# One block inversion moved from VectorE to GpSimd, its follow-up steps pinned in the issue order, and the filler work dealt out anew, in a two-layer hybrid transformer kernel

## Chip, cores and metric

One core of a Trainium2 chip. The metric is the device time of one launch in microseconds (us), taken on the slowest core, here the only one. Inputs and outputs are float32; the weights are read from HBM once per launch.

## What is computed

Two layers over 256 latent tokens and 256 context tokens, model width 1024. Each layer has a modulation (six vectors out of one matrix product with the conditioning), a mixer of three branches (A: delta rule, B: gated linear attention, C: differential attention), a gated merge, and a feed-forward part (dense in layer 0, eight experts in layer 1). Cut to what matters here:

```python
mod_l = jnp.split((silu(c) @ w_mod[l] + b_mod[l])[:, None, :], 6, axis=-1)   # and mod_c from c_ctx
hl = _modulate(xl, norm1_g[l], mod_l[0], mod_l[1])
...
# branch A, per head and chunk of 64 tokens
lmat = jnp.tril(jnp.einsum('bhnid,bhnjd->bhnij', kb, k) * decay, -1)
tinv = lax.linalg.triangular_solve(eye + lmat, eye, left_side=True, lower=True, unit_diagonal=True)
u = tinv @ (v * beta)
w = tinv @ (kb * jnp.exp(gc)[..., None])
...
# merge
(ga * (ya @ w_o_a) + gb * (yb @ w_o_b) + gd * (yd @ w_o_c)) @ w_out          # gates: sigmoid(h @ w_in part)
```

What the change is about is `tinv`, the inverse of a unit lower triangular 64x64 matrix, of which a layer needs many.

## The kernel before

**Matmuls.** Every large product is made three times over (`mm3`, L272 to L274): both operands are split into a high and a low part, and high by high, high by low and low by high are summed in PSUM. A weight tile of 1 MB is loaded into one of three "raw" buffers (`load`, L248); its high part is a cast on ScalarE (ACT, L267), its low part a subtraction on VectorE (DVE, L268), four pieces of 128x512 to a load, put in a ring called "hl" (tiles `whl`). One load feeds two groups of 24 matmuls, of 512 columns where both token halves are wanted and of 256 where only the latents are (layer 1's gates).

**The order of the work.** A scheduler lays out the program by the order in which the code asks for things, one queue per engine, each carried out in its order. In `mixer` that order is a string, `PLAN` (L27, L28), one for each layer. Its words are stages: "pr" prepares the delta rule (matrices U, one for each direction), "iv" inverts (`a_inv`), "sc" is its scan, "gaN", "gbN", "gcN" are N loads' worth of the sigmoid gates of the three branches, computed ahead and parked in HBM, "za" the output gate of branch A, "qkB", "vB", "dec", "gla" branch B, "qC", "kC", "vC", "dif" branch C, "ha" to "hc" the heads' outputs and "ma" to "mc" the merges. "mN" stands for N units of modulation for later use.

**Modulation units.** `mod_unit` loads 1 MB of `w_mod` into a raw buffer and runs 8 matmuls on it (L348; 16 records in the trace) without a split, so its raw buffer is free only when the matmuls are done. Four units make a group in one PSUM tile; `mod_put` then copies the tile (ACT, L356, `modr`), transposes it by two matmuls (L359) and adds the bias (DVE, L366). The generator `mods` (L364 on) deals out the units; with `behind=0` a group's `mod_put` stands right behind its last unit. At the start of the program `run` takes eight units in groups of two, tag "c" (tile `rawc`), and between them the squares and row sums of the two token halves x (`norm_only`, L420 to L425, L432).

**The inversion.** `a_inv` gathers the 32x32 diagonal blocks of all matrices of a layer in one tile (128 partitions, 32x32), L642 and L644, makes N of them (L648) and solves by 31 steps of substitution (L653 a product, L655 a subtraction, over at most 256 elements a partition, in place in Y). Then it puts the result together: a copy (L657), a predicated copy (L658), two transposes (L659, L660), four copies back to U on ACT and four on DVE (L665, L667), a memset of Q on GpSimd (POOL, L669) and eight copies into Q (L675, L677). `a_join` (L680 on) goes from blocks of 32 to 64 by small matmuls (L699 on), and the scan follows.

The functions that the diff touches, as they stood:

Of the kernel before, what the change touches and what calls it, by code (L numbers as in the profile page):

```python
# [2 lines left out]

# [1 line left out]

# [18 lines left out]
MOE_RAW = (1, 0, 0)  # L24
MOE_PART = 3
PRE = (7,)
PLAN = ("sm ap su pr iv ga4 m4 za sc m16 dec qkB gb1 ha ma vB gla qC kC m4 gc1 vC hb dif mb hc mc",  # L27
        "sm ap pr ga1 m8 iv sc za m6 ga3 m1 gc1 qkB dec vB ha ma gla qC kC m1 vC hb dif mb hc mc")  # L28
MOE_PRE = 9
MOE_AT = 0  # L30
PART = 512
# [165 lines left out]
class Prog:  # L197
# [44 lines left out]
    def load(self, src, shape, tag="raw"):  # L242
# [5 lines left out]
        self.nc.sync.dma_start(r, src.rearrange("p (a b) -> p a b", a=n))  # L248
        return r

    def part(self, v):

        nc = self.nc
        n, size = v.shape[1], v.shape[2]
        step = -(-n // -(-n * size // PART))
        H, L = [], []
        for k in range(0, n, step):
            m = min(step, n - k)
            t = self.st.tile([128, 2, m, size], F32R, name="whl", tag="hl", bufs=2 * N_HL)
            self.split(t[:, 0], t[:, 1], v[:, k:k + m])  # L260
            H += [t[:, 0, i] for i in range(m)]
            L += [t[:, 1, i] for i in range(m)]
        return H, L
# [104 lines left out]
    def mods(self, groups, tag="raw", behind=1):  # L368

        last = []  # L370
        for l, us in groups:
            p = self.pm()
            for i, u in enumerate(us):
                self.mod_unit(l, u, i, len(us), p, tag)
                if i < len(us) - 1:
                    yield
            last.append((l, us, p))
            if len(last) > behind:
                self.mod_put(*last.pop(0))
            yield  # L380
        for v in last:
            self.mod_put(*v)

# [244 lines left out]
    def a_inv(self, s):  # L628

        nc = self.nc  # L630
        U = s["U"]
        W1 = self.ch([2, 32, 32], "W1")
        W2 = self.ch([2, 32, 32], "W2")
        Dg, M, N, Y = W1[:, 0], W1[:, 1], W2[:, 0], W2[:, 1]
        nc.gpsimd.memset(Y, 0.0)
        nc.gpsimd.memset(Y.rearrange("p i j -> p (i j)")[:, 0:1024:33], 1.0)
        quad = [slice(b * 32, (b + 1) * 32) for b in range(4)]
        for d in range(2):
            for b, r in enumerate(quad):
                src, dst = U[d][r, :, r], Dg[r, :, 16 * d:16 * d + 16].rearrange("p i m -> p m i")  # L640
                if b % 2:
                    nc.vector.tensor_copy(dst, src)  # L642
                else:
                    nc.scalar.copy(dst, src)  # L644
        nc.vector.transpose(M, Dg)
        dmb = self.dmask[:, :, None].to_broadcast([128, 32, 32])
        nc.scalar.copy(N, M)
        nc.vector.copy_predicated(N, dmb, M.rearrange("p i j -> p j i"))  # L648
        for c in range(31):
            a, b = 31 - c, c + 1  # L650
            tmp = self.sm([512], "fs")
            tv = tmp[:, :a * b].rearrange("p (a b) -> p a b", a=a)
            nc.vector.tensor_mul(tv, N[:, c + 1:, c:c + 1].to_broadcast([128, a, b]),  # L653
                                 Y[:, c:c + 1, :b].to_broadcast([128, a, b]))
            nc.vector.tensor_sub(Y[:, c + 1:, :b], Y[:, c + 1:, :b], tv)  # L655
        Z, Ps, Qs = M, Dg, N
        nc.scalar.copy(Z, Y)  # L657
        nc.vector.copy_predicated(Z, dmb, Y.rearrange("p i j -> p j i"))  # L658
        nc.vector.transpose(Ps, Z)  # L659
        nc.vector.transpose(Qs, Z.rearrange("p i j -> p j i"))  # L660
        for d in range(2):
            for b, r in enumerate(quad):
                dst, src = U[d][r, :, r], Ps[r, :, 16 * d:16 * d + 16].rearrange("p i m -> p m i")
                if b % 2:
                    nc.vector.tensor_copy(dst, src)  # L665
                else:
                    nc.scalar.copy(dst, src)  # L667
        Q = W1.rearrange("p a i j -> p (a i j)").rearrange("p (d m j) -> p d m j", d=2, m=16)
        nc.gpsimd.memset(Q, 0.0)  # L669
        for d in range(2):  # L670
            for b, r in enumerate(quad):
                c = slice((b % 2) * 32, (b % 2) * 32 + 32)
                dst, src = Q[r, d, :, c], Qs[r, :, 16 * d:16 * d + 16].rearrange("p i m -> p m i")
                if b % 2:
                    nc.vector.tensor_copy(dst, src)  # L675
                else:
                    nc.scalar.copy(dst, src)  # L677
        self.a_join(U, Q)

    def a_join(self, U, Q):  # L680

# [758 lines left out]
    def mixer(self, l, H):  # L1440

        self.todo = self.mods(MOD_AHEAD[l], behind=0)
        T, m = {}, []
        gn = lambda n: self.P(f"gn{n}{l}") if n != "c" else self.A["gnc", l]
        zu = {"a": U_ZA, "b": U_RB, "c": None}
        for w in PLAN[l].split():
            if w == "su":
                self.setup2()
            elif w == "sm":
                self.small_proj(l, H)  # L1450
            elif w == "ap":
                self.a_proj(l, H)
            elif w == "pr":
                T["s"] = self.a_prep(l)
            elif w == "iv":
                self.a_inv(T["s"])
            elif w == "sc":
                T["oa"] = self.a_scan(l, T["s"])
            elif w == "qkB":
                T[w] = self.gla_qk(l, H)  # L1460
            elif w in ("vB", "vC"):
                T[w] = self.values(l, U_VB if w == "vB" else U_VC, H, w)
            elif w == "dec":
                self.gla_decays(l)
            elif w == "gla":
                T["ob"] = self.gla(l, T["qkB"], T["vB"])
            elif w == "qC":
                T[w] = self.diff_qk(l, H, w, U_QC, 256 * l, 0.125)
            elif w == "kC":
                T[w] = self.diff_qk(l, H, w, U_KC, 0, 1.0)  # L1470
            elif w == "dif":
                T["oc"] = self.diff(l, T["qC"], T["kC"], T["vC"])
            elif w[0] == "z":
                self.stashed[l, w] = self.z_ahead(l, zu[w[1]], H, gn(w[1]), w[1])
            elif w[0] == "g":
                self.gates_ahead(l, "abc".index(w[1]), H, int(w[2:] or 4))
            elif w[0] == "h":
                T["y" + w[1]] = self.head_out(l, T["o" + w[1]], gn(w[1]), H, zu[w[1]], w[1])
            elif w in ("ma", "mb", "mc"):
                first = not m  # L1480
                m = m or self.wide(l, "m")
                self.merge(l, "abc".index(w[1]), H, T["y" + w[1]], m, first)
            else:
                for _ in range(int(w[1:])):
                    next(self.todo, None)
        return m
# [86 lines left out]
```

## Time and profile before

| what | value |
| --- | --- |
| median of 3 runs | 2606.64 us (2603.16 to 2609.61) |
| the profiled execution | 2607.5 us, its span 2605.7 us |
| PE (TensorE) busy | 2455.8 us, 94% of the span |
| DVE busy | 1718.3 us, 66% |
| ACT busy | 1417.3 us, 54% |
| POOL busy | 87.6 us, 3% |
| read from HBM | 463.65 MB, 181 GB/s over the span |
| mean granted clock of PE | 0.962 of full |

Busy time is the sum over an engine's instructions. Times inside the span count from its start. An engine's idle time costs something only if PE, or what PE waits for, is behind it. The granted clock of a stretch is 1.00 at the higher level (2.4 GHz) and 0.50 at the lower (1.2 GHz); between them the stretch had some of each.

### The profile page before, as it was taken

Reading aid. Unit: us, or ns where it says so; the run is one execution under the profiler, and the core shown is the slowest. Engines: PE = TensorE matmul, PEld = TensorE weight load, DVE = VectorE, ACT = ScalarE, POOL = GpSimd, SP = SyncE. Lnnn points to the kernel's source line nnn. Section 1 sums busy time; section 2 is a strip of 40 time slices with the busy share of each in tenths; the row PEclk is TensorE's granted clock in tenths of the full one; section 3 lists DMA queues with packets and bytes.
Section 4 is the critical chain, followed back from the end, with each engine's and each line's share of the span. In section 5 each row is a group of like instructions: output and inputs, shape, how many; then the busy total and the mean of one; then the engine's idle time right before and its main releaser. Section 6 shows DMA issues by size and latency. Waiting matters only on the chain.

```text
span 2605.7 us, 35872 instructions
## 1 busy us (share of the span) xinstructions
PE 2455.8 (94%) x13712; PEld 1979.8 (76%) x13712; DVE 1718.3 (66%) x3130; ACT 1417.3 (54%) x2352; POOL 87.6 (3%) x216
## 2 busy tenths in 40 slices
PE   5998999999998999998979999998999999999997
PEld 3786777677677788886859878787878888878876
DVE  4675446655644533335686475767988888988987
ACT  3764343225553432334845432666878777777775
POOL 0000001110010000000000010010000000000000
PEclk8998999989999999998978999998999999999998
DMA  6323632022132223222273130246979899999994
GB/s 248 110 93 149 246 132 71 17 106 81 49 128 83 81 77 121 96 74 89 97 271 115 46 141 33 89 169 261 386 270 365 332 350 351 346 347 353 342 366 181
DMA packets 72707, 473.13 MB, mean 182 GB/s; under 512 B 8208, under 2 KB 10384, under 8 KB 19664
## 3 DMA queue, kind: packets, MB, share of 16 engines
q1 hardware_dynamic: 68208, 464.73, 48.1%
q10 hardware_dynamic: 4320, 6.03, 0.6%
q8 instruction: 110, 1.80, 0.3%
q14 instruction: 69, 0.57, 0.1%
HBM read 463.65 MB, written 7.08 MB: 181 GB/s over the span
## 4 chain that ended last, share of the span: by engine, by line
PE 85%; DVE 8%; ACT 4%; issue 2%; DMA 1%; SPq 0%; POOL 0%; ACTq 0%; DVEq 0%; POOLq 0%
PE pm L273 19%; PE pm L272 19%; PE pm L274 19%; PE y L274 3%; PE y L273 3%; PE y L272 3%; PE la L985 2%; PE pm L348 2%; PE pq L1052 1%; DVE ATb L987 1%; PE pm L844 1%; PE ob L996 1%; PE tp L1352 1%; DMA raw<-in_wmod_dram 1%; DVE zq L973 1%
## 5 line engine op out<-in xcount | busy, mean ns | idle before, releaser
L268 DVE TENSOR_TENSOR whl<-raw,whl 128x512 fp32r<-128x512 f32 (+2 forms) x490 | 331.2, 682 | 341.0 <-ACT whl L267 338.0
L272 PE MATMUL pm<-hh,whl 128*128 128x512 f32 (+2 forms) x1264 | 477.7, 380 | 13.0 <-ACT whl L267 6.6
L274 PE MATMUL pm<-hh,whl 128*128 128x512 f32 (+2 forms) x1264 | 467.7, 371 | 12.3 <-DVE whl L268 12.3
L267 ACT CAST whl<-raw 128x512 fp32r<-128x512 f32 (+2 forms) x490 | 289.8, 600 | 339.9 <-PE pm L274 268.7
L273 PE MATMUL pm<-hl,whl 128*128 128x512 f32 (+2 forms) x1264 | 470.9, 373 | 0.0
L268 DVE TENSOR_TENSOR wp<-rawc,wp 128x1024 fp32r<-128x1024 f32 x261 | 313.6, 1222 | 36.7 <-ACT wp L267 30.6
L272 PEld LDWEIGHTS pm<-hh,whl 128*128 128x128 f32 (+1 forms) x1264 | 244.8, 194 | 60.6 <-ACT whl L267 8.6
L274 PEld LDWEIGHTS pm<-hh,whl 128*128 128x128 f32 (+1 forms) x1264 | 243.5, 193 | 54.8 <-DVE whl L268 14.3
L267 ACT CAST wp<-rawc 128x1024 fp32r<-128x1024 f32 x261 | 268.1, 1051 | 21.1 <-PE y L274 11.5
L273 PEld LDWEIGHTS pm<-hl,whl 128*128 128x128 f32 (+1 forms) x1264 | 244.7, 194 | 42.6 <-issue 6.3
L268 DVE TENSOR_TENSOR wlo<-raw,whi 128x1024 fp32r<-128x1024 f32 x176 | 210.0, 1222 | 34.1 <-ACT whi L267 31.6
L273 PE MATMUL pm<-wlo,hg 128*128 128x512 f32 x530 | 211.8, 400 | 1.6 <-DVE wlo L268 1.4
L272 PE MATMUL pm<-whi,hg 128*128 128x512 f32 x530 | 211.2, 398 | 0.0
L274 PE MATMUL pm<-whi,hg 128*128 128x512 f32 x530 | 207.7, 392 | 0.0
L267 ACT CAST whi<-raw 128x1024 fp32r<-128x1024 f32 x176 | 179.0, 1052 | 13.2 <-PE pm L273 11.9
L273 PE MATMUL y<-wp,mt 128*128 128x512 f32 x348 | 135.4, 389 | 0.0
L274 PE MATMUL y<-wp,mt 128*128 128x512 f32 x348 | 135.3, 389 | 0.0
L273 PEld LDWEIGHTS pm<-wlo,hg 128*128 128x128 f32 x530 | 99.7, 188 | 34.6 <-DVE wlo L268 15.8
L272 PE MATMUL y<-wp,mt 128*128 128x512 f32 x348 | 120.1, 389 | 0.2 <-ACT mt L1354 0.2
L272 PEld LDWEIGHTS pm<-whi,hg 128*128 128x128 f32 x530 | 99.7, 188 | 20.9 <-ACT hg L1328 0.2
L274 PEld LDWEIGHTS pm<-whi,hg 128*128 128x128 f32 x530 | 99.7, 188 | 20.2
L268 DVE TENSOR_TENSOR wlo<-rawc,whi 128x1024 fp32r<-128x1024 f32 x91 | 110.9, 1219 | 1.9 <-ACT whi L267 1.3
(394 smaller groups left out, 4542.8 us busy)
## 6 DMA issues: line engine op xcount, KB each, us to landing
rawc<-in_m_dram SPq DMA_DIRECT2D x176, 1024.0 KB, 6.0
raw<-in_m_dram SPq DMA_DIRECT2D x88, 1024.0 KB, 7.4
raw<-in_win_dram SPq DMA_DIRECT2D x64, 1024.0 KB, 4.9
raw<-in_wmod_dram SPq DMA_DIRECT2D x40, 1024.0 KB, 5.0
raw<-in_f_dram SPq DMA_DIRECT2D x22, 1024.0 KB, 4.8
raw<-in_wo_dram SPq DMA_DIRECT2D x24, 512.0 KB, 3.7
raw<-in_f_dram SPq DMA_DIRECT2D x16, 704.0 KB, 4.0
rawc<-in_wmod_dram SPq DMA_DIRECT2D x8, 1024.0 KB, 16.9
```

What stands on the lines that cost most here:

```text
L267: self.nc.scalar.copy(hi, src)
L268: self.nc.vector.tensor_sub(lo, src, hi.bitcast(F32))
L272: mm(p, wh, ah, start=first, stop=False)
L273: mm(p, wh, al, start=False, stop=False)
L274: mm(p, wl, ah, start=False, stop=last)
L348: nc.tensor.matmul(p[j:j + 32, :256], self.cs[:, k, o:o + 32], w[:, k], start=i == 0 and k < 4, stop=i == n - 1 and k >= 4)
L844: nc.tensor.matmul(ps[:, :n], self.ones, sq[:, :n], start=True, stop=True)
L973: nc.vector.tensor_mul(FQ[hp][r, x, a].rearrange("p (n s) -> p n s", s=LEVELS[li]), side(Fj[:, x]), side(q[hp]))
L985: mm(p[:, x % 2, hp], FK[hp][:, x], FQ[hp][:, x], start=True, stop=True)
L987: nc.vector.copy_predicated(AT.rearrange("p h a (n t s) -> p (h a) n t s", t=2, s=s)[:, :, :, 1 - d], mk[:, None].to_broadcast([128, 4, 64 ...
L996: mm(o[:, hp], vB[:, tt, h * 128:(h + 1) * 128], AT[:, hp, a], start=True, stop=first)
L1052: mm(p[:, :nk], q[ms, h, cs], k[ms, h, :nk], start=True, stop=True)
```

## The change

Three things. (1) The 62 instructions of the substitution run on POOL instead of DVE, in both layers. (2) `a_inv` ends behind them; putting together ("jo", new function `a_blocks`) and joining ("jn") are stages of their own, held behind the last instruction that PE, DVE and ACT (for "jn": PE) had been given until then (`behind`); in the plans the gates, the output gate "za" and four modulation units come before "jo", and the other fillers stand elsewhere. (3) `mods` now puts a group away after the next group's first unit. Line numbers in the new file are larger by 1 to 25.

```diff
+    @contextmanager
+    def behind(self, *engines):
+        last = {}
+        for i in self.nc.cur_bb.bb.instructions:
+            last[i.engine] = i
+        with ExitStack() as es:
+            for e in engines:
+                es.enter_context(self.tc.issue_after(last[getattr(mybir.EngineType, e)]))
+            yield
...
-PLAN = ("sm ap su pr iv ga4 m4 za sc m16 dec qkB gb1 ha ma vB gla qC kC m4 gc1 vC hb dif mb hc mc",
-        "sm ap pr ga1 m8 iv sc za m6 ga3 m1 gc1 qkB dec vB ha ma gla qC kC m1 vC hb dif mb hc mc")
+PLAN = ("sm ap su pr iv ga4 za m4 jo gb1 jn gb1 sc m8 qkB dec ha vB ma gla qC kC m8 gc1 vC hb dif mb hc m4 mc",
+        "sm ap pr iv ga4 za gb3 m4 jo gb1 gc1 jn gc1 sc m4 qkB dec vB ha ma gla qC kC m4 vC hb dif mb hc m4 mc")
...
             for i, u in enumerate(us):
                 self.mod_unit(l, u, i, len(us), p, tag)
-                if i < len(us) - 1:
-                    yield
+                if len(last) > behind:
+                    self.mod_put(*last.pop(0))
+                yield
             last.append((l, us, p))
-            if len(last) > behind:
-                self.mod_put(*last.pop(0))
-            yield
...
-            nc.vector.tensor_mul(tv, N[:, c + 1:, c:c + 1].to_broadcast([128, a, b]),
+            nc.gpsimd.tensor_mul(tv, N[:, c + 1:, c:c + 1].to_broadcast([128, a, b]),
                                  Y[:, c:c + 1, :b].to_broadcast([128, a, b]))
-            nc.vector.tensor_sub(Y[:, c + 1:, :b], Y[:, c + 1:, :b], tv)
-        Z, Ps, Qs = M, Dg, N
+            nc.gpsimd.tensor_sub(Y[:, c + 1:, :b], Y[:, c + 1:, :b], tv)
+        s["inv"] = W1, W2
+
+    def a_blocks(self, s):
+        U = s["U"]
+        W1, W2 = s["inv"]
+        ...
+        Z, Ps, Qs = W1[:, 1], W1[:, 0], W2[:, 0]
...
-        self.a_join(U, Q)
+        s["Q"] = Q
...
+            elif w == "jo":
+                with self.behind("PE", "DVE", "Activation"):
+                    self.a_blocks(T["s"])
+            elif w == "jn":
+                with self.behind("PE"):
+                    self.a_join(T["s"]["U"], T["s"]["Q"])
```

How the order moves, at three places. First ACT at the very start of the program (x_97 and x_98 are the two token halves). Before:

```order
L356 COPY modr<-pm 128x256
L420 ACTIVATE sq<-x_97 128x512 x4
L410 ACTIVATE rs<-pq,cb 128x256
L420 ACTIVATE sq<-x_98 128x512
L411 ACTIVATE rs<-rs,cb 128x256
L420 ACTIVATE sq<-x_98 128x512 x3
L457 ACTIVATE hh<-x_97,mod_84,A_171 128x256 x2
```

Changed:

```order
L429 ACTIVATE sq<-x_97 128x512 x4
L419 ACTIVATE rs<-pq,cb 128x256
L420 ACTIVATE rs<-rs,cb 128x256
L367 COPY modr<-pm 128x256
L429 ACTIVATE sq<-x_98 128x512 x4
L419 ACTIVATE rs<-pq,cb 128x256
L420 ACTIVATE rs<-rs,cb 128x256
L367 COPY modr<-pm 128x256 x2
```

The copy of the first modulation group, which waits for two units' matmuls, no longer stands ahead of the squares of x.

Second, DVE in layer 0 around the end of the inversion (W_1172 and W_1173 are the tiles that hold the blocks, U_950 and U_951 the matrices, `whl` a weight's split). Before:

```order
L268 TENSOR_TENSOR whl<-raw,whl 128x512 x2
L658 COPY_PREDICATED W_1172<-mk,W_1173 128x1024
L268 TENSOR_TENSOR whl<-raw,whl 128x512
L659 STREAM_TRANSPOSE W_1172<-W_1172 128x1024
L660 STREAM_TRANSPOSE W_1173<-W_1172 128x1024
L665 COPY U_950<-W_1172 32x16x32 x2
L665 COPY U_951<-W_1172 32x16x32 x2
L268 TENSOR_TENSOR whl<-raw,whl 128x512 x4
L675 COPY W_1172<-W_1173 32x16x32 x4
L807 SCALAR_TENSOR_TENSOR zs<-pm,par,zs 128x512
```

Changed:

```order
L279 TENSOR_TENSOR whl<-raw,whl 128x512 x8
L826 SCALAR_TENSOR_TENSOR zs<-pm,par,zs 128x512 x4
L677 COPY_PREDICATED W_1172<-mk,W_1173 128x1024
L678 STREAM_TRANSPOSE W_1172<-W_1172 128x1024
L679 STREAM_TRANSPOSE W_1173<-W_1172 128x1024
L684 COPY U_950<-W_1172 32x16x32 x2
L684 COPY U_951<-W_1172 32x16x32 x2
L279 TENSOR_TENSOR whl<-raw,whl 128x512 x3
L694 COPY W_1172<-W_1173 32x16x32 x4
```

All of "za" (eight splits, four `zs`) now stands ahead of the putting together; the splits for "gb1" (the three behind it) stand behind it, and DVE carries them out only after L677 to L684, which wait for POOL.

Third, SP, the queue that issues the loads, at the end of layer 0 (`raw<-in_wo` and `raw<-in_win` are weights of the merge, `raw<-g` a parked gate). Before:

```order
L234 DMA raw<-g_4804 128x1024
L248 DMA raw<-in_wo_dram 128x1024
L248 DMA raw<-in_win_dram 128x2048
L248 DMA raw<-in_wo_dram 128x1024
L248 DMA raw<-in_win_dram 128x2048
L1437 DMA x_6510<-in_x_dram 128x2048
L1437 DMA x_6511<-in_x_dram 128x2048
L248 DMA raw<-in_wo_dram 128x1024
L248 DMA raw<-in_win_dram 128x2048
```

Changed:

```order
L248 DMA raw<-in_wmod_dram 128x2048 x3
L1456 DMA x_6505<-in_x_dram 128x2048
L1456 DMA x_6506<-in_x_dram 128x2048
L248 DMA raw<-in_wmod_dram 128x2048
L234 DMA raw<-g_4823 128x1024
L248 DMA raw<-in_wo_dram 128x1024
L248 DMA raw<-in_win_dram 128x2048
```

Four modulation units now stand in the ring of raw buffers ahead of the last merge's weights.

## Rows read from the trace of the kernel before

**Rows 1.** The page, chain that ended last: shares of the span by engine.

```profile
PE 85%; DVE 8%; ACT 4%; issue 2%; DMA 1%; SPq 0%; POOL 0%; ACTq 0%; DVEq 0%; POOLq 0%
```

**Rows 2.** Timeline of PE, start of the program (start us, duration us, what).

```profile
29.78 2.07 PE L425 MATMUL pq<-sq,ones 128*128 128x256 f32 x4 [4.41 <-DVE sq L423]
...
42.84 0.61 PE L359 MATMUL pm<-cstt,modr 128*128 128x4 f32 x4 [0.49 <-ACT modr L356]
47.67 0.66 PE L272 MATMUL pm<-hh,whl 128*48 128x512 f32 x1 [4.22 <-ACT whl L267]
```

**Rows 3.** Timeline of ACT, the same stretch.

```profile
17.34 0.37 ACT L356 COPY modr<-pm 128x256 f32<-128x256 f32 x1 [11.46 <-PE pm L348]
```

**Rows 4.** DMA view, window 0 to 32 us: everything moved in it.

```profile
DMA packets 1899, 12.42 MB, mean 388 GB/s; under 512 B 203, under 2 KB 363, under 8 KB 491
```

**Rows 5.** Windows of layer 0: busy us of PE, PEld, DVE, ACT, POOL; clock; DMA.

```profile
200.00:210.00 10.00, 5.05 (x16) 3.59 (x13) 9.42 (x27) 4.58 (x8) 0.00 (x0) 0.50 0.60 247
210.00:220.00 10.00, 9.54 (x36) 7.38 (x34) 9.87 (x14) 7.89 (x11) 1.81 (x1) 0.85 0.29 105
```

**Rows 6.** Timeline of PE in layer 0, 190 to 201 us.

```profile
191.61 0.39 PE L273 MATMUL pm<-hl,whl 128*128 128x512 f32 x1
191.83 0.39 PE L274 MATMUL pm<-hh,whl 128*128 128x512 f32 x1
192.15 2.80 PE L348 MATMUL pm<-raw,cs 128*32 128x256 f32 x48
198.69 1.44 PE L348 MATMUL pm<-raw,cs 128*32 128x256 f32 x16 [3.75 <-DMA raw<-in_wmod_dram]
```

**Rows 7.** One window of layer 1 (columns as in rows 5).

```profile
1330.00:1340.00 10.00, 6.28 (x33) 6.28 (x33) 9.93 (x18) 6.29 (x10) 0.00 (x0) 0.53 0.24 90
```

**Rows 8.** First join matmuls: source view of tile v, layer 0, then layer 1.

```profile
L699 PE MATMUL v<-W,U x128: 191/191/212, 220.8 to 223.8; 32*32 32x32 f32 x128
...
L699 PE MATMUL v<-W,U x192: 191/194/365, 1386.9 to 1397.4; 32*32 32x32 f32 x128, 64*64 64x64 f32 x64
```

**Rows 9.** Groups of DVE, 183 to 208 us: busy, mean ns | idle before.

```profile
L653 DVE TENSOR_TENSOR fs<-W 128x31 f32<-128x31 f32 (+15 forms) x31 | 10.6, 343 | 1.1
```

**Rows 10.** POOL: two groups of the whole span, then two single instructions.

```profile
L1112 POOL TENSOR_TENSOR m<-m,sg 128x512 f32<-128x512 f32 x12 | 19.2, 1599 | 118.2 <-DVE sg L1111 92.5 <-DVE r L1059 19.7 <-DVE r L1054 6.0
L1112 POOL TENSOR_TENSOR m<-m,sg 128x256 f32<-128x256 f32 x14 | 13.5, 966 | 124.3 <-issue 63.1 <-DVE sg L1111 57.7 <-DVE r L1054 3.4
...
723.45 1.29 POOL L1112 TENSOR_TENSOR m<-m,sg 128x512 f32<-128x512 f32 x1 [23.85 <-DVE sg L1111]
...
1695.25 0.74 POOL L1112 TENSOR_TENSOR m<-m,sg 128x256 f32<-128x256 f32 x1 [12.81 <-DVE sg L1111]
```

**Rows 11.** Groups of the putting together, 208 to 228 us.

```profile
L667 ACT COPY U<-W 32x512 f32<-32x512 f32 x4 | 4.6, 1147 | 0.0
L677 ACT COPY W<-W 32x512 f32<-32x512 f32 x4 | 4.3, 1077 | 0.1
...
L267 ACT CAST whl<-raw 128x512 fp32r<-128x512 f32 x5 | 2.9, 617 | 2.0 <-PE pm L274 2.0
...
L658 DVE COPY_PREDICATED W<-mk,W 128x1024 f32<-128x1024 uint8 x1 | 2.0, 2017 | 0.0
...
L669 POOL MEMSET W<- 128x2048 f32 x1 | 1.8, 1815 | 72.3 <-ACT U L667 72.3
...
L659 DVE STREAM_TRANSPOSE W<-W 128x1024 f32<-128x1024 f32 x1 | 1.2, 1246 | 0.0
L657 ACT COPY W<-W 128x1024 f32<-128x1024 f32 x1 | 1.0, 1045 | 3.9 <-DVE W L655 3.9
```

**Rows 12.** The page, DMA issues: KB each, median us from issue to landing.

```profile
raw<-in_wmod_dram SPq DMA_DIRECT2D x40, 1024.0 KB, 5.0
```

**Rows 13.** Timeline of PE at the end of layer 0, before the last merge.

```profile
735.14 1.42 PE L272 MATMUL pm<-yh,whl 128*128 128x512 f32 x1
```

**Rows 14.** Timeline of DVE: the first substitution step of layer 0.

```profile
183.51 0.21 DVE L653 TENSOR_TENSOR fs<-W 128x31 f32<-128x31 f32 x1
```

More of the change, by code (lines that the diff above doesn't have):

```diff
@@ L1 @@
 import math
-from contextlib import ExitStack
+from contextlib import ExitStack, contextmanager
 import numpy as np
@@ L652, in a_inv @@
             tv = tmp[:, :a * b].rearrange("p (a b) -> p a b", a=a)
-            nc.vector.tensor_mul(tv, N[:, c + 1:, c:c + 1].to_broadcast([128, a, b]),
+            nc.gpsimd.tensor_mul(tv, N[:, c + 1:, c:c + 1].to_broadcast([128, a, b]),
                                  Y[:, c:c + 1, :b].to_broadcast([128, a, b]))
-            nc.vector.tensor_sub(Y[:, c + 1:, :b], Y[:, c + 1:, :b], tv)
-        Z, Ps, Qs = M, Dg, N
+            nc.gpsimd.tensor_sub(Y[:, c + 1:, :b], Y[:, c + 1:, :b], tv)
+        s["inv"] = W1, W2
+    def a_blocks(self, s):
+        nc = self.nc
+        U = s["U"]
+        W1, W2 = s["inv"]
+        quad = [slice(b * 32, (b + 1) * 32) for b in range(4)]
+        dmb = self.dmask[:, :, None].to_broadcast([128, 32, 32])
+        Y = W2[:, 1]
+        Z, Ps, Qs = W1[:, 1], W1[:, 0], W2[:, 0]
         nc.scalar.copy(Z, Y)
```

## Prediction

> **What bounds the kernel now.** The chain that ended last comes first: 85% of it is PE, 8% DVE, 4% ACT, 1% DMA [rows 1]. So nearly everywhere the end is set by PE's own work, and an edit that only moves work of DVE, ACT or POOL is worth what PE waits for in its place. The change adds no matmul of weight and takes none away; what can move the time is PE's idle time and the stretches at its lower clock behind it. I looked for these with the windows and PE's timeline, at the five places where the order changes: the program's start, the inversions of layers 0 and 1, and the two ends of the mixers.
>
> At the start PE waits 4.41 us for the squares of the second half of x, and the last modulation group is put away at 42.84, so that the first projection starts at 47.67 [rows 2]. ACT had stood idle for 11.46 us before the copy of the first group, with the squares queued behind that copy [rows 3]. In layer 0, PE was busy for 5.05 us of the ten from 200 to 210, at the lower clock, and the ten after that had a granted clock of 0.85 [rows 5]: it waits first for the fourth of four modulation units, 3.75 us [rows 6], then for weight splits that stand on DVE among the substitution. Layer 1 shows the same: DVE 9.93 busy, PE 6.28 at a clock of 0.53 [rows 7]. The join starts at 220.8 in layer 0 and at 1386.9 in layer 1 [rows 8].
>
> **The start.** The order shows the squares ahead of the copy, so x no longer waits for the second unit's matmuls, and PE's waits for squares and for `modr` go. What is left is the loading: constants, two halves of x and eight units, 10.9 MB, at the 388 GB/s of [rows 4], are in by some 28 us, and 30 with what else is in the queue. The eighth unit takes 1.9 us at the lower clock (2.80 for three at the higher [rows 6], 0.93 each, doubled) and the copy 0.5, so the last transposes start at about 32.5 in place of 42.84. Ends: 10 us if all of that reaches the first projection, nothing if the mul and split work of the norm on DVE sets it anyway. I take 9, since the stretch from the last transpose to the projection, 4.8 us, stays as it is. **+9.**
>
> **Putting groups away later.** Each group's transposes waited 0.49 us for the copy [rows 2]. Ten later groups hold 4.9 us of it at most, and most stand where PE waits for something else as well. **+1.5.**
>
> **The substitution on POOL.** No row shows it there. There are 62 instructions; step c covers (31-c)(c+1) elements, 5456 over the steps and 10912 with both instructions. From below: DVE's own price, 62 x 0.343 = 21.3 us, and 0.036 between two of them (1.1 over 31), 23.5 us in all [rows 9]. From POOL's own rows: a two-input instruction took 1.29 us for 512 elements and 0.74 for 256 when alone, hence 2.15 ns an element and 0.19 fixed; the means over all are 1.60 and 0.97, hence 2.47 ns and 0.33 [rows 10]. That gives 23.5 + 11.8 + 2.2 = 37.5 us alone, and 27.0 + 20.6 + 2.2 = 49.8 us if every one is as disturbed as the mean. In the stretch DVE has only eight splits and four `zs` in layer 0, so I take 41, nearer to the row alone.
>
> Here a rule of the Trainium skill speaks against the change: GPSIMD Engine Reference, sections 1 and 3, has a two-input elementwise operation at 1.96 times VectorE's time, and the two engines share SBUF interfaces, so that each holds up the other when DVE reads two inputs. The spread between 1.29 and the mean of 1.60 us [rows 10] fits it; by its ratio on DVE's 21.3 us the substitution would be an estimated 44 us with the gaps, and the sum 6 us later than mine.
>
> **Layer 0's inversion.** It starts at 183.5 [rows 14] and ends on POOL at 224.5. Behind it come copy, predicated copy, transpose and four copies on ACT, 1.0 + 2.0 + 1.2 + 4.6 [rows 11], then the cast of "gb1", 0.6: PE can go on at 233.9. It covers the time with the four groups of "za", 24 matmuls each that start 0.22 to 0.23 us apart [rows 6], 5.5 us a group, from 192.1 to 214; then four units at 0.93 each (2.80 for three [rows 6]), whose fourth load starts only when the first buffer is free, lands 5.0 us later [rows 12], and ends PE's work at 221. PE idles from 221 to 234, runs two groups of "gb1" (11 us), and pays for the lower clock: after the idle stretch of [rows 5] it was at that level for the rest of that window and 30% of the next (0.85), some 5.5 us of work, or 2.8 us lost. The join starts at 247.7. Up to there the order holds 302 matmuls of 512 columns instead of 201, 23 us more work, so the old start of 220.8 [rows 8] is worth 243.8 on this scale. **-4**, and one for one with POOL's time: +13 at the lower bound, -13 at the upper.
>
> DVE's freed 24 us are worth nothing of their own: they let the splits of "za" run early, which is what the 214 stands on. POOL's later memset (1.8) and the copies into Q (4.3) end before 247 and are hidden by the two groups.
>
> **Layer 1's inversion.** There DVE is full where N is made [rows 7], and in the old order the substitution waited among splits; I put POOL's start at 1336 and its end at 1377. Copies into Q now stand ahead of the casts, so the path is 8.8 + 1.8 + 4.3 + 0.6 [rows 11], to 1392.5; four groups of 256 columns (half of 5.5 each) and 2.8 for the clock bring the join to 1406.3. The order holds 263 more matmuls of 256 columns (30 us) and ten units fewer (80 matmuls, 9 us) ahead of it: 1386.9 [rows 8] is worth 1408. **+2**, again one for one with POOL.
>
> **Modulation units elsewhere.** A unit keeps its raw buffer until PE has used it. At the end of each layer four of them stand ahead of the last merge's weights in that ring. The merge started at 735.14 in layer 0 [rows 13]. Now the first unit is done at about 737, the fourth load lands at 742 (5.0), the merge's weight of half the size comes behind it (half of 5.0, in part beside it) and is split: 745. Of the ten us later, 3.7 are the units' own work that no longer stands elsewhere. Ends: 6 lost, or nothing, if the units fill the wait ahead of the merge. **-5** in layer 0, and by the same order **-5** in layer 1. Eight instead of four units in branch B: five loads wait for a buffer, three at a time, beside 7.5 us of their matmuls and the branch's own; between 0 and -8, **-1** taken, as PE has other work there.
>
> **Sum.** 9 + 1.5 - 4 + 2 - 5 - 5 - 1 = -2.5: the profiled execution of 2607.5 us becomes **2610**. That execution is 0.9 above the median of 2606.6, so this is 0.13% above the median, inside the 0.3% (7.8 us) that a measurement of this kernel can tell from no change.
>
> **Rivals.**
> - *POOL is the bound (slower).* If DVE's splits disturb POOL as in the mean of [rows 10], each inversion ends 9 us later, and PE, out of work at 221 in layer 0, waits for all of it: 2610 + 18 = 2628. It decides from a substitution of about 44 us on. For it: the two means, and that layer 1 has more splits in the stretch. Against it: the single rows at 1.29 and 0.74. The same side is reached, at 2619, if the start is set by DVE and gives nothing.
> - *The units are cover, not delay (faster).* If the units ahead of the last merges fill time in which PE would wait for the head's norm, the 10 us come back: 2600, and with a substitution of 37.5 us 2593. For it: PE does wait ahead of that merge. Against it: they stand behind the norm's row sums in PE's order.
> - *The change does not do what it says.* The pins hold a_blocks behind work that is late itself, so that POOL's end is not what starts them; then "za" is on the path and the substitution's place is worth nothing, leaving start and units: about 2608. It counts with the middle.
>
> **Chances.** The middle (forecast, or parts that cancel), within 0.3%: 0.37. The first rival and smaller relatives, slower by more: 0.34. The second with a good start, faster by more: 0.29. The range takes in 2593 and 2628 and a little beyond at either end: 2589 to 2631. The middle's own range is 2602 to 2614.
>
> **What would show it.** First projection at 38 to 39 us: the start. POOL's first TENSOR_TENSOR to last at 41 us per layer, with a single 256-element instruction at 0.74 to 0.97: the price. PE idle of about 13 us ahead of "gb1" in layer 0, ended by ACT or DVE `whl`: the path. A wait of PE for `raw` or `whl` ahead of the last merge in both layers: the units. A substitution over 46 us, or a last merge that starts no later than its units' work explains, makes the forecast wrong.

## The result and the profile after

The changed kernel takes 2677.07 us, the median of 4 runs (2663.74 to 2683.99), against 2604.97 for the kernel before: 1.0273 times as long, with a 95% interval of 1.0251 to 1.0295. The prediction said 2610, in a range of 2589 to 2631, so it is wrong by 67 us. The profiled execution took 2676.04 us, its span 2674.2; all places below are from it.

The page first, PE's busy time and the chain that ended last:

```profile
PE 2471.8 (92%) x13712; PEld 1987.4 (74%) x13712; DVE 1678.0 (63%) x3006; ACT 1417.2 (53%) x2352; POOL 161.5 (6%) x340
...
PE 83%; DVE 6%; ACT 5%; POOL 3%; issue 2%; DMA 1%; SPq 0%; ACTq 0%; DVEq 0%; POOLq 0%
```

PE has the same 13712 instructions. Its share of the chain fell from 85% [rows 1] to 83%, POOL's rose from 0 to 3%: about 80 us of the span, so POOL now is on the path. That alone does not say where the 70 us went, since both inversions waited for DVE before.

To find the places, time was set against work. Each PE instruction counts with the usual distance to its successor in the kernel before (0.227 us for 512 columns, 0.120 for 256, 0.110 for 128, and so on by size; the 30th percentile of each size); the 16 records of a modulation unit count 0.93 us together, as three units took 2.80 [rows 6]. The clock time at which a kernel has done so much work, less that work, is what PE has lost until then, by idle time and by the lower clock. It is counted from PE's first matmul to its last. Both kernels hold 2243 us of work, so the differences between them are differences of loss. By stretches of work done, us; the first line is what the kernel before lost in it, the others are more (+) or less (-) than that:

```
work done        0-130 130-215 215-548 548-608 608-1075 1075-1195 1195-1395 1395-1435 1435-   all
before            38.9    32.1    81.2    12.6     30.9      50.1      46.2       8.7  43.1
after            -11.7    -0.4    +6.2   +26.1     -1.2      +4.5      +9.1     +36.6  -0.9 +68.3
e1_units         -10.2    -2.3   +12.3   +23.8     -2.3      +5.5      +5.2     +30.7  -2.2 +60.7
e2_gates         -11.3    -1.7    +3.7    +7.2     -2.0     +10.3     +12.1      +8.1  -1.7 +24.7
e3_dve           -10.4    -6.7    +5.2   +26.5     -2.5     -11.3      +7.8     +37.2  -0.3 +45.5
e4_late          -11.7    +6.0   -10.7    +0.2     -2.2      -4.6      +4.4      +0.4  -2.2 -20.5
e5_late_pool     -11.1   +23.4    -4.9    +1.1     -1.9     +16.3      +2.8      +0.6  -1.8 +24.7
e6_late_gates    -11.6    +5.7    -1.6    +1.2     -1.9      -2.5      -3.3     +37.1  -2.0 +21.0
e7_gates_dve     -12.0    -7.0    +7.9    +6.7     -1.2      +0.4     +12.0      +7.8  -1.8 +12.8
e8_mix           -11.7    -7.9   -10.6    +0.3     -2.2      -4.3      +2.8      +0.6  -1.7 -34.6
e9_pin1          -11.8    -6.1    -8.8    +0.3     -2.3      +5.1      +4.7      +0.3  -1.7 -20.4
e10_gate_b        -9.8    -6.7    -6.5   +23.7     -1.8      -2.8      +1.3      +0.4  -1.8  -3.8
e11_m8           -11.7    -5.8    -1.7    +0.3     -1.2      -2.9      +1.5      -0.3  -2.0 -23.8
e12_order        -11.1    -5.4    -2.1    +0.3     -2.3      -4.7      +3.2      +0.5  -1.5 -23.1
```

The stretches are: the start; layer 0's inversion and scan; its branch B and most of its attention; the attention's end and the last merge; the feed-forward part and layer 1's projections; layer 1's inversion; its scan, branch B and attention; the end of that attention and the last merge; the rest. Each line is one profiled execution. In 215 to 548 the spread between executions is large: e4 and e6 have the same instructions in the same order there and differ by 9 us. In the two stretches with last merges, which this document rests on, the kernels fall into three groups with nothing between: up to 1.2 us, 6.7 to 8.1, and 23.7 to 37.2.

So the new kernel wins 12 us at the start, loses 4 at the two inversions, 63 at the ends of the two attentions, and 15 in the stretches ahead of these (215 to 548 and 1195 to 1395). PE's windows at layer 0's end and layer 1's (start:end, length, then busy us of PE, PEld, DVE, ACT, POOL, PE's granted clock, DMA share, GB/s), before:

```profile
710.00:730.00 20.00, 16.83 (x74) 11.14 (x72) 10.20 (x20) 11.49 (x24) 2.99 (x2) 1.00 0.11 33
...
1680.00:1700.00 20.00, 18.03 (x136) 15.40 (x135) 14.75 (x35) 13.07 (x30) 2.59 (x3) 1.00 0.16 44
1700.00:1720.00 20.00, 16.43 (x104) 14.96 (x104) 10.18 (x20) 12.95 (x31) 3.00 (x4) 0.83 0.35 127
```

and after:

```profile
710.00:730.00 20.00, 12.36 (x38) 7.09 (x38) 6.31 (x17) 4.49 (x12) 0.09 (x1) 0.63 0.21 79
730.00:750.00 20.00, 12.69 (x60) 4.23 (x60) 5.78 (x10) 10.40 (x18) 0.00 (x0) 0.61 0.13 43
...
1730.00:1750.00 20.00, 12.21 (x51) 7.25 (x49) 8.24 (x22) 4.29 (x10) 2.53 (x3) 0.73 0.16 54
1750.00:1770.00 20.00, 12.76 (x32) 7.00 (x32) 4.25 (x11) 5.68 (x14) 0.00 (x0) 0.50 0.00 0
```

For 40 us in each layer PE is busy some 12 us of 20, at a clock of 0.50 to 0.73; before, it was busy 17 to 18 of 20 at 1.00 around the attention's end (721.7 and 1699.9), and 16.4 at 0.83 behind it in layer 1. The last 20 us before 1770 are at the lower level (1.2 GHz) throughout. Where the attention ends is told by its products with the values (`oc`; source view of its line, first and last start), before in both layers, then after:

```profile
L1069 PE MATMUL oc<-PT,vC x96: 270/275/377, 620.9 to 721.7; 128*128 128x128 f32 x96
L1069 PE MATMUL oc<-PT,vC x64: 275/275/377, 1646.8 to 1699.9; 128*128 128x128 f32 x64
...
L1088 PE MATMUL oc<-PT,vC x96: 270/275/582, 622.4 to 729.5; 128*128 128x128 f32 x96
L1088 PE MATMUL oc<-PT,vC x64: 272/275/581, 1691.4 to 1764.5; 128*128 128x128 f32 x64
```

From the first to the last it takes 101 us before and 107 after in layer 0, and 53 and 73 in layer 1. Who is waited for there (PE's waits: us in total, times, longest; after, 1690 to 1790, and then before, 1640 to 1720):

```profile
PE tp L1084 <- DVE e L1081: 11.6, 5, 4.2
PE pm L863 <- ACT sq L861: 5.2, 5, 1.6
PE pm L283 <- ACT whl L278: 2.4, 1, 2.4
PE pm L359 <- DMA raw<-in_wmod_dram: 1.8, 1, 1.8
...
PE tp L1065 <- DVE e L1062: 2.7, 4, 0.8
```

The first is the attention's own chain: scores, softmax on ACT and DVE (`e`), transposes `tp`. PE waited for it before too, but for 2.7 us. The waits that the prediction put at this place, for a unit's load and for the merge's first split, are 4.2 us in layer 1, and 2.1 and 2.5 us in layer 0.

At the inversions, POOL's first and last steps and three in between, layer 0 and then layer 1 (start us, us):

```profile
171.96 0.56 POOL L662 TENSOR_TENSOR fs<-W 128x31 f32<-128x31 f32 x1 [38.60 <-DVE W L657]
...
178.90 0.92 POOL L662 TENSOR_TENSOR fs<-W 128x175 f32<-128x175 f32 x1
179.90 0.53 POOL L664 TENSOR_TENSOR W<-W,fs 128x175 f32<-128x175 f32 x1
...
205.86 0.49 POOL L662 TENSOR_TENSOR fs<-W 128x175 f32<-128x175 f32 x1
...
212.02 0.25 POOL L664 TENSOR_TENSOR W<-W,fs 128x31 f32<-128x31 f32 x1
...
1356.05 0.57 POOL L662 TENSOR_TENSOR fs<-W 128x31 f32<-128x31 f32 x1 [34.54 <-DVE W L657]
...
1400.63 0.25 POOL L664 TENSOR_TENSOR W<-W,fs 128x31 f32<-128x31 f32 x1
```

That is 40.3 and 44.8 us, 41 forecast. PE's one long wait behind it in layer 0 (waits, 180 to 240), and then the first join matmuls of each layer (view of tile v):

```profile
PE pm L283 <- ACT whl L278: 12.0, 1, 12.0
```

```profile
L718 PE MATMUL v<-W,U x192: 191/194/312, 235.2 to 245.5; 32*32 32x32 f32 x128, 64*64 64x64 f32 x64
...
L718 PE MATMUL v<-W,U x192: 191/194/365, 1427.6 to 1441.8; 32*32 32x32 f32 x128, 64*64 64x64 f32 x64
```

### The profile page after: what moved, and what is told of

Its sections match the earlier page's. It is cut to its first block, busy times and chain, and to the rows that moved or that the text cites. A ratio compares the mean times of both kernels' runs of the same rounds, so it can differ in the third digit from the quotient of the medians.

```text
span 2674.2 us, 35919 instructions
## 1 busy us (share of the span) xinstructions
PE 2471.8 (92%) x13712; PEld 1987.4 (74%) x13712; DVE 1678.0 (63%) x3006; ACT 1417.2 (53%) x2352; POOL 161.5 (6%) x340
## 4 chain that ended last, share of the span: by engine, by line
PE 83%; DVE 6%; ACT 5%; POOL 3%; issue 2%; DMA 1%; SPq 0%; ACTq 0%; DVEq 0%; POOLq 0%
PE pm L283 19%; PE pm L284 19%; PE pm L285 19%; PE y L285 3%; PE y L284 3%; PE y L283 3%; PE la L1004 2%; PE pq L1071 1%; POOL W L664 1%; PE pm L359 1%; POOL fs L662 1%; PE pm L863 1%; PE oc L1088 1%; PE ob L1015 1%; PE ob L1017 1%
## 5 line engine op out<-in xcount | busy, mean ns | idle before, releaser
L279 DVE TENSOR_TENSOR wp<-rawc,wp 128x1024 fp32r<-128x1024 f32 x261 | 313.5, 1221 | 36.7 <-ACT wp L278 30.6
L285 PEld LDWEIGHTS pm<-hh,whl 128*128 128x128 f32 (+1 forms) x1264 | 242.3, 192 | 49.3 <-DVE whl L279 12.5
L284 PEld LDWEIGHTS pm<-wlo,hg 128*128 128x128 f32 x530 | 99.8, 188 | 34.6 <-DVE wlo L279 15.8
```

The costliest lines, as they stand in the source:

```text
L279: self.nc.vector.tensor_sub(lo, src, hi.bitcast(F32))
L284: mm(p, wh, al, start=False, stop=False)
L285: mm(p, wl, ah, start=False, stop=last)
```

## The experiments

Two theories for the ends of the attentions. **P, the plug**: the four units ahead of the last merge hold all raw buffers, so no filler (other work that PE could do in a wait) can be loaded. **G, gates used up**: gate matmuls that the new plans compute early are the work that used to fill the attention's waits. And one question beside: what POOL costs.

**The units moved away (e1), the gates given back (e2), the substitution on VectorE (e3), the late putting away alone (e4).** All four ran on one chip, in three rounds. Edits to the changed kernel for e1 to e3; e4 is the kernel before with the new `mods`.

```diff
 e1_units: layer 0, then layer 1
-... sc m8 qkB ... hb dif mb hc m4 mc
+... sc m12 qkB ... hb dif mb hc mc
-... sc m4 qkB ... hb dif mb hc m4 mc
+... sc m8 qkB ... hb dif mb hc mc
 e2_gates: layer 0, then layer 1
-... jo gb1 jn gb1 sc m8 ...
+... jo gb1 jn sc m8 ...
-... iv ga4 za gb3 m4 jo gb1 gc1 jn gc1 sc m4 ...
+... iv ga4 za m4 jo gc1 jn sc m4 ...
 e3_dve
-            nc.gpsimd.tensor_mul(tv, N[:, c + 1:, c:c + 1].to_broadcast([128, a, b]),
+            nc.vector.tensor_mul(tv, N[:, c + 1:, c:c + 1].to_broadcast([128, a, b]),
-            nc.gpsimd.tensor_sub(Y[:, c + 1:, :b], Y[:, c + 1:, :b], tv)
+            nc.vector.tensor_sub(Y[:, c + 1:, :b], Y[:, c + 1:, :b], tv)
```

> The changed kernel (2676 us) with one edit: the four modulation units that stood ahead of each layer's last merge are computed in the scan of branch A instead. Theory P (plug): these units hold all three raw buffers until PE reaches them, which is behind the attention and its norm, so every weight load behind them waits and the attention's last stretch has no filler; then both last merges come back to within some 3 us of the old kernel, 18 us back in layer 0 and 25 to 30 in layer 1, and the time is 2628 to 2638 us. Theory G (gates used up): the gates that were computed ahead at the inversions are missing as filler in the attention; then only the units' own waits go, some 6 us a layer, and the time is 2660 to 2667 us, with the attention of layer 1 still idle and at the lower clock.

> The changed kernel with the gates given back: layer 0 without the second gb1, layer 1 without gb3, gb1 and the second gc1; the four units ahead of each last merge stay. Theory P: the last merges lose as much as in the changed kernel (some 20 us in layer 0, 31 in layer 1), since the loads of these gates stand behind the units in the ring; the time stays within 10 us of 2676. Theory G: the attention of layer 1 has its fillers back, its last merge loses less than 12 us, and the time falls to 2650 or less, less whatever the inversion of layer 1 then loses.

> The changed kernel with the substitution back on VectorE, all else as changed. By the prediction's sum POOL's 41 us against 23.5 on VectorE cost little in the end: the same to 15 us a layer that PE would else not wait, so 2640 to 2676 us. If the substitution on POOL is what made the kernel slow, both inversions gain 17 us or more and the time falls to 2640 or below, while the last merges still lose their 20 and 31 us. If it is not, the last merges keep the loss and the time stays above 2650.

> The kernel before with one edit: a modulation group is put away after the next group's first unit. Every theory: the first projection starts about 10 us earlier as in the changed kernel, and nothing else moves much: 2592 to 2598 us. If the earlier start is lost again further on, 2605.

Measured: e1 2662.42 us (1.0215 of before, 1.0198 to 1.0232), e2 2632.81 (1.0116, 1.0097 to 1.0135), e3 2652.78 (1.0185, 1.0168 to 1.0202), e4 2590.90 (0.9951, 0.9933 to 0.9968).

P falls as the main cause. With the units gone from the place, e1 still loses 23.8 and 30.7 us there, of 26.1 and 36.6, and its time lies in the range that G gave (2660 to 2667). PE's windows in layer 1's attention (e1, 1750 to 1770):

```profile
1750.00:1760.00 10.00, 6.58 (x16) 3.29 (x16) 3.06 (x8) 2.14 (x5) 0.00 (x0) 0.50 0.00 0
1760.00:1770.00 10.00, 5.85 (x16) 3.32 (x16) 3.35 (x9) 2.29 (x6) 0.00 (x0) 0.50 0.00 0
```

No buffer is held by units here, and DMA moves nothing: SP issues no load from 1742 to 1788; what is in line there are the last merge's weights, and that merge needs the attention's result. e2 keeps the units where they were and gives the gates back: its last merges lose 7.2 and 8.1 us instead of 26.1 and 36.6, and the longest wait of PE for the softmax in layer 0 goes from 3.4 us to 0.6. G holds. The units cost something as well: 2.3 and 5.9 us go with them in e1, and e2 and e7, which have them but not the early gates, lose 6.7 to 8.1 us where kernels with neither lose at most 1.2.

e2 shows the other side as well. With fewer gates ahead of it, layer 1's inversion has too little to cover POOL (e2, PE's waits, 1335 to 1440):

```profile
PE pm L283 <- ACT whl L278: 28.9, 1, 28.9
```

e3 prices POOL: 24 us less than the changed kernel, 6.3 of them in layer 0's inversion and 15.8 in layer 1's. The same wait in layer 0 is then 5.5 us instead of 12.0. The last merges keep their loss, so the two causes are separate. e4 is faster than the kernel before, by 1 us more than its range; in the profiled execution it has won 11.7 us by the end of the start, and the medians differ by 13.6.

**The converse: causes added to a kernel without the others (e5, e6), and both taken away (e7).** e5 and e6 start from e4, e7 from e2; e8 mixes. One chip, three rounds.

```diff
 e5_late_pool: nc.vector.tensor_mul, tensor_sub of the substitution -> nc.gpsimd, in the order of before
 e6_late_gates: layer 1
-... sc za m6 ga3 m1 gc1 qkB ...
+... sc za m6 ga3 gb4 m1 gc2 qkB ...
 e7_gates_dve: e2 with nc.vector in the substitution
 e8_mix: nc.vector in the substitution, and the changed kernel's plans replaced
+"sm ap su pr iv ga4 za m4 jo gb1 jn sc m16 dec qkB ha ma vB gla qC kC m4 gc1 vC hb dif mb hc mc"
+"sm ap pr ga1 m8 iv jo jn sc za m6 ga3 m1 gc1 qkB dec vB ha ma gla qC kC m1 vC hb dif mb hc mc"
```

> The kernel with only the late putting away (2591 us), and the substitution on GpSimd, in the old order and without pins. If GpSimd's longer time is on the path, both inversions end later by most of the 17 us that 41 takes over 24, and the time is 2608 to 2625 us. If the fillers of the old order hide it, or VectorE's freedom to split early pays for it, 2585 to 2595.

> The kernel with only the late putting away (2591 us), and in layer 1 four loads of gate b and a second one of gate c computed ahead, in the scan of branch A; substitution on VectorE, no pins, no units ahead of the last merges. Theory G (gates used up early leave the attention without filler): the last merge of layer 1 loses 20 to 30 us as in the changed kernel, the scan gains little, and the time is 2606 to 2621 us. If the loss at the last merge comes from the units, the pins or GpSimd, the time stays within 6 us of 2591.

> The kernel with the gates given back (2633 us), and the substitution on VectorE. The two causes add up: less by the 24 us that the substitution's place made in the changed kernel, or more, since PE there waited 28.9 us in one piece for the first split behind the inversion of layer 1: 2600 to 2612 us. If with fewer gates ahead GpSimd's time were hidden, 2625 or more.

> Late putting away, substitution on VectorE, layer 1 as in the kernel before, and layer 0's inversion in the changed order (za and four units ahead of the pinned steps, one gb1 between them and the join), all else of layer 0 as before. If the pins are worth something once the substitution is short, layer 0's inversion ends some 5 us earlier by work done: 2583 to 2588 us. If not, as the late putting away alone, 2591, or slower by up to 5.

Measured: e5 2629.47 us (1.0083, 1.0060 to 1.0105), e6 2628.48 (1.0071, 1.0049 to 1.0093), e7 2618.76 (1.0042, 1.0031 to 1.0054), e8 2576.04 (0.9885, 0.9856 to 0.9914).

e6 has no GpSimd, no pins, no units ahead of a merge, and loses 37.1 us at layer 1's last merge. The windows of the attention's last 40 us, e4 and then e6, and the products with the values in each:

```profile
1640.00:1660.00 20.00, 19.18 (x125) 14.75 (x124) 13.78 (x27) 10.77 (x25) 2.20 (x3) 1.00 0.32 107
1660.00:1680.00 20.00, 19.26 (x133) 15.54 (x132) 14.80 (x35) 12.34 (x29) 2.62 (x3) 1.00 0.12 40
...
1700.00:1720.00 20.00, 12.38 (x30) 5.55 (x28) 6.23 (x16) 4.28 (x10) 0.00 (x0) 0.50 0.00 0
1720.00:1740.00 20.00, 11.42 (x30) 6.34 (x29) 5.20 (x13) 7.22 (x19) 0.00 (x0) 0.50 0.00 0
```

```profile
L1067 PE MATMUL oc<-PT,vC x64: 273/275/377, 1625.8 to 1680.0; 128*128 128x128 f32 x64
...
L1067 PE MATMUL oc<-PT,vC x64: 273/399/583, 1666.0 to 1731.4; 128*128 128x128 f32 x64
```

The five loads of gates that were taken from it are 10 groups of 24 matmuls of 256 columns, 29 us of PE at the higher clock. Their absence costs more than that: with less for PE to do in between, the attention takes 65 us instead of 54, and its matmuls get longer (median 399 ns against 275) at a granted clock of 0.50. Done early, the gates win 7.7 us in the stretch 1195 to 1395, where they went; the medians of e6 and e4 differ by 37.6, and e6 is 7.5 us above its range.

e5 puts the price of POOL at 38.6 us where the order gives it no cover: 17.4 in layer 0's inversion, the 17 that 41 takes over 24, and 20.9 in layer 1's; the whole is 4.5 us above its range. PE's waits in layer 0 (160 to 235) and in layer 1 (1290 to 1400):

```profile
PE pm L272 <- ACT whl L267: 29.2, 1, 29.2
...
PE pm L272 <- ACT whl L267: 26.7, 2, 24.6
```

e7, with both causes gone, is 14 us better than e2, less than the 24 I expected, and still slower than the kernel before. It missed its range by 7 us; what is left in it stands at the last merges (6.7 and 7.8, with the units still there), in 215 to 548 and in 1195 to 1395. e8 does better than I expected: layer 0's inversion in the new order is worth 14 us (-7.9 against e4's +6.0) once the substitution is short, and the kernel is 1.15% faster than the one before.

**What is left: pins in layer 1 (e9), one gate load in layer 0 (e10), branch B's fillers (e11) and order (e12).** Each from e8, three rounds.

```diff
 e9_pin1: layer 1
-... ga1 m8 iv jo jn sc za m6 ...
+... ga1 m4 iv za m4 jo jn sc m6 ...
 e10_gate_b: layer 0
-... jo gb1 jn sc m16 ...
+... jo gb1 jn gb1 sc m16 ...
 e11_m8: layer 0
-... sc m16 dec qkB ha ma vB gla qC kC m4 gc1 ...
+... sc m12 dec qkB ha ma vB gla qC kC m8 gc1 ...
 e12_order: layer 0
-... sc m16 dec qkB ha ma vB gla ...
+... sc m16 qkB dec ha vB ma gla ...
```

> The mixed kernel (2576 us), and layer 1's inversion in the changed manner too: za and four of the eight units between the inversion and its pinned steps, substitution on VectorE, gates as before. If ordering the steps behind the fillers is what layer 0 gained from, layer 1 gains some 10 us as well: 2562 to 2568 us. If its gain there came from the cover alone, which layer 1 has less of, 2574 to 2582.

> The mixed kernel (2576 us), and a second load of gate b of layer 0 computed ahead, between the join and the scan; nothing on GpSimd, no units ahead of the last merges. If one load's gates used up early (two groups, 11 us of PE) are what layer 0's last merge lost 20 us by, that place loses 12 to 22 us here and the whole 5 to 20: 2581 to 2596 us. If the order of the work there does not matter, 2572 to 2580.

> The mixed kernel (2576 us), with four of the sixteen units of layer 0's scan moved into branch B (eight there, as in the changed kernel). Between layer 0's scan and its attention the changed kernel lost 6 us against the old one where the kernels with four units there gained 10 to 12. If the eight units are the cause (three buffers, each held until PE is through), this loses 8 to 18 us: 2584 to 2594. If they find cover there, as my prediction had it, 2574 to 2580.

> The mixed kernel (2576 us), with branch B's stages of layer 0 in the changed kernel's order (qkB ahead of dec, vB ahead of ma). If this order is the cause of the loss between scan and attention, 2584 to 2594; if not, 2572 to 2580.

Measured: e9 2588.23 us (0.9940, 0.9919 to 0.9960), e10 2605.04 (1.0003, 0.9989 to 1.0016), e11 2585.65 (0.9921, 0.9904 to 0.9938), e12 2587.92 (0.9938, 0.9919 to 0.9958).

e10 is the cleanest piece: one load's worth of gate b, two groups or 11 us of PE, moved from the attention to the place behind the join, costs 29 us in all and 23.4 at layer 0's last merge, 9 and 1 us more than expected. The last 20 us of the attention in e8, the window of that end in e10, and the products with the values in e8 and e10:

```profile
670.00:680.00 10.00, 9.41 (x46) 6.36 (x46) 6.17 (x15) 6.04 (x14) 0.00 (x0) 1.00 0.46 159
680.00:690.00 10.00, 9.47 (x44) 6.26 (x42) 5.81 (x15) 5.03 (x12) 0.00 (x0) 1.00 0.00 0
...
710.00:730.00 20.00, 12.11 (x27) 5.78 (x26) 3.95 (x10) 6.18 (x12) 0.00 (x0) 0.50 0.15 52
...
L1088 PE MATMUL oc<-PT,vC x96: 270/275/377, 590.2 to 691.0; 128*128 128x128 f32 x96
L1088 PE MATMUL oc<-PT,vC x96: 270/275/582, 609.8 to 721.7; 128*128 128x128 f32 x96
```

PE's wait for the softmax there (waits, 680 to 750):

```profile
PE tp L1084 <- DVE e L1081: 9.6, 3, 3.4
```

In e8 that wait is 0.5 us (680 to 730). The attention takes 101 us in e8 and 112 in e10, with 11 us of work less around it. The move won nothing where it went: from 130 to 548 e10's execution is 5 us worse than e8's. e9 misses on both counts, it is slower by 12 us, 9.4 of them in layer 1's inversion: with four units less ahead of it and za ahead of the pins, PE waits 7.4 us for Q at the join (0.2 in e8) and 5.9 us for VectorE's reading of za's results (`zs`, none in e8). e11 and e12 are slower than e8 by 10 and 12 us by the medians, each in its range, and by 9 in 215 to 548, by one execution each. As that stretch differed by 9 us between two executions of the same order, and e11's interval overlaps e8's, e11 is not clear of noise; which waits they lengthen was not settled. e8's own four runs spread from 2570.9 to 2582.3.

## Why the prediction was wrong

**The start: right.** +10.5 forecast for the two terms together, 11.7 by the table. The first projection, at 47.67 [rows 2], comes at 38.89; the range 38 to 39 was named. The last transposes start at 34.64, 2 us later than put. On the timeline of PE, the row sums of the first half of x, the last transposes and that projection:

```profile
13.92 2.08 PE L434 MATMUL pq<-sq,ones 128*128 128x256 f32 x4 [3.98 <-DVE sq L432]
...
34.64 1.02 PE L370 MATMUL pm<-cstt,modr 128*128 128x4 f32 x4 [1.90 <-ACT modr L367]
38.89 0.66 PE L283 MATMUL pm<-hh,whl 128*48 128x512 f32 x1 [3.23 <-ACT whl L278]
```

**POOL's price: right.** 41 us forecast, 40.3 and 44.8 measured; both between the 37.5 alone and the 49.8 of a disturbed one. The rule that I had weighed, the Trainium skill's GPSIMD Engine Reference, section 3, with its 1.96, is borne out as a rough size: POOL was busy 35.6 us for layer 0's substitution and 40.0 for layer 1's, against 21.3 on VectorE [rows 9], 1.7 and 1.9 times. What does not hold is that the kernel pays for POOL's time one for one: on VectorE, among its splits, layer 0's substitution took 27.8 us from its first step to its last (e3), 12.5 less, and PE's wait fell by 6.5.

**Layer 0's inversion: right.** PE's wait was forecast at 12.9 us and is 12.0. The join, set at 247.7 on the old scale, starts at 235.2 in a kernel that is 11.7 us ahead, 246.9: 3 us behind its worth of 243.8. By the end of the scan that is won back (-0.4 for the stretch); the 4 lost were forecast up to the join only.

**Layer 1's inversion: nearly right to the join, short behind it.** POOL starts at 1356.05 in a kernel that is 19 us late, so at 1337 (1336 was put); the join at 1427.6, which is 1408.6 on that scale, 1406.3 forecast, with POOL 3.8 us over its 41. But the stretch costs 4.5 us where a gain of 2 was forecast. From the join's start to the scan's first matmul it was 12.6 us before (1386.9 to 1399.46) and is 21.8 now (1427.6 to 1449.44); 5.2 of the 9.2 more are work, the gates of one load of c, and 4 are loss. The new plan leaves the join that load for company, where the old one had za and six units: in the window from 1430 to 1440 PE is busy 5.65 us at a clock of 0.59. In it is one wait of 3.95 us for which the profile names no releaser.

**The step that failed** is the credit for gates done early: the place that they are taken from has no term in the sum. In layer 1, "The order holds 263 more matmuls of 256 columns (30 us)" counts them one for one, as if what comes later got shorter by as much (the traces show 274). 192 of them are four loads of gate b (1056 matmuls of 256 columns are ahead of the join in the changed kernel, 864 in e2); a second load of gate c, behind the join, stands in no term. In layer 0 the credit of 23 us is not what failed: e8 has the same matmuls ahead of its join and loses 0.3 us at the last merge. There it is the second "gb1", behind the join, for which the sum has nothing, and which alone makes the loss (e10). The share of 85% [rows 1] was taken to hold everywhere, and no windows of the attention were read. There the bound is the chain of scores, softmax and transposes, and the gate and merge matmuls are its cover. With two groups fewer in layer 0 and ten in layer 1 PE idles in the chain's waits, the granted clock goes to 0.50, and the chain itself takes longer. Without the units (e1) that costs 23.8 us for 11 us of gates in layer 0 (23.4 in e10) and 30.7 for 29 in layer 1 (36.7 in e6 against e4).

**The units ahead of the last merge: about right.** -5 each was forecast. Taking them away from the changed kernel gives back 2.3 and 5.9 us at that place (e1; 15 in all by the medians), and where the gates are in place the merges lose 6.7 to 8.1 us with the units and at most 1.2 without. The waits named for it are there, 4.6 us in layer 0 and 4.2 in layer 1. The second rival, that the units are cover, is not borne out.

**Branch B: too small.** -1 was taken for eight units in place of four. e11 has that alone and is 10 us slower than e8, not clear of noise; the new order of the branch's stages had no term, and e12, with that alone, is 12 us slower.

**The first rival, POOL as the bound,** did not come as put: 40.3 and 44.8 us, not 50. Its threshold of about 44 was reached in layer 1, where it explains 3.8 us. That POOL stands in VectorE's place costs 24 us in this order (e3), but the forecast counted with 41 us of it. The fillers hid part of it; in the old order its price is 38.6 us (e5).

Undone one at a time, then, of the 72 us by medians: the gates 44 (e2), POOL 24 (e3), the units 15 (e1). These overlap, since the gates were there to cover POOL: with gates and POOL both undone (e7) 58 are gone, not 68. Branch B's part was measured on another kernel (e8) and cannot be added to them. Against all this stand 14 won by the late putting away (e4).

## What to carry to other kernels

Filler work that is moved ahead to cover a wait is taken from another wait: before it is credited, look at the windows of the stretch that it leaves, and ask what bounds that stretch without it. A place where PE is over 90% busy and waits little (e8, 670 to 690) can be one whose own chain is the bound and only looks like PE's. There a us of filler taken away cost more than a us (23 for 11, 31 to 37 for 29), as PE idled and the rest ran at the lower clock. And slower work on a spare engine is free only as far as there is filler that nobody else needs.

## What was not expected of the hardware

In e1, e6 and the changed kernel PE's granted clock stood at 0.50, the lower level, for 30 to 40 us on end in layer 1's attention (1750 to 1780, 1700 to 1740, 1740 to 1770), while PE was busy 56 to 71% of the time. The attention's own PE work takes about twice its time at that level, and it is part of the chain. Eight products with the values near the end of layer 0's attention, in e8 at a clock of 1.00, and in e10 at 0.50:

```profile
690.16 1.10 PE L1088 MATMUL oc<-PT,vC 128*128 128x128 f32 x8
...
710.69 2.07 PE L1088 MATMUL oc<-PT,vC 128*128 128x128 f32 x8
```

On GpSimd a two-input step took 0.92 us for 175 elements at 178.90, beside one of VectorE's splits; the subtraction of as many right behind it took 0.53, and the product of 175 at 205.86 took 0.49, both with VectorE idle. VectorE pays too: its eight splits during layer 0's substitution took 0.742 us on the mean, against 0.684 for the three in the same stretch before. That the two engines share their access to SBUF is what the Trainium skill's GPSIMD Engine Reference has in section 1, and these rows agree.

The same instructions in the same order (e4 and e6, layer 0) differed by 9 us over branch B and the attention between two executions, more than the whole effect of some edits; the runs of the changed kernel spread over 20 us, those of the kernel before over 6.
